# Weights 64 and 16 bytes past a multiple of 256 in a float32 decoder kernel

## The chip, the cores and the metric

The kernel runs on one core of a Trainium2 chip. The metric is the device time of one execution in microseconds. A core's engines work side by side and wait for one another by semaphores: TensorE (PE; PEld is its weight load), VectorE (DVE), ScalarE (ACT), GpSimd (POOL), and SyncE (SP), which here only issues transfers.

## The reference

A decoder trunk of two layers over 256 positions of width 2048, in float32. Cut to what matters here:

```python
h = _rmsnorm(x, nrm[0])
proj = h @ w_in_a[layer]                 # queries, keys, values; layer B has its own
...                                      # dilated windows (A) or stick-breaking (B), plus memory attention
x = x + _rmsnorm(heads @ w_o, norms[1])
u = _rmsnorm(x, norms[2]) @ w_up         # 2048 x 11264
gate, val = jnp.split(u, 2, axis=-1)
...                                      # causal convolution of width 3 on gate
f = (jax.nn.silu(acc) * val) @ w_down    # 5632 x 2048
x = x + _rmsnorm(f, norms[3])
```

Nearly all of the work is products of the 256 rows with large weight matrices, which are read from HBM once.

## The kernel before, in words

Each float32 operand is split into a high part, rounded to TensorE's `float32r`, and a low part, the rest. A product is then high x high + low x high + high x low, three matmuls. `split` makes the parts: ScalarE copies the loaded weights `raw` to `whi` (line 660), VectorE subtracts that from `raw` to `wlo` (line 661). Each pair of tiles holds 1024 columns of weights; there are four buffers of each.

Two forms of matmul use them, and in both a weight load (of the stationary operand, 128 columns) goes ahead of each matmul (which streams the moving operand).

In the activation-stationary form (`as_mm`, `mm3`, line 128) the weights move: 512 columns of `whi` or `wlo` stream past 128 columns of activations. It serves the values, the output and down projections, and, in `wide`, sums of blocks of weights (`forms`, tile `x`) and of activations.

In the weight-stationary form (`ws_mm`, line 145) 128 columns of `whi` or `wlo` are loaded and the activations move. `h` holds high and low parts of a block of 128 features side by side, so that one matmul of 512 columns gives high x high and high x low; one of 256 columns then gives low x high. A tile of 128 output features takes 16 such pairs. The weight-stationary tiles come in three places:

- `ws_tile`: 60 tiles, one after the other (queries, keys, the first group of the gated MLP and others); sums go to `ps_g`.
- `ws_beside`: 96 tiles, one in each unit of `wide`. A unit multiplies seven products of the activation-stationary form and one such tile, in halves of eight pairs between the products, pinned in program order. There are twelve stages of `wide` with eight units each. Sums go to `ps_s`.
- `mem_kv`: 64 pairs at the start, on weights from `piece`.

The program's order is written out by hand: `later` queues a step for a later tile, `behind_this` for the rest of a unit, and `pin` keeps what it wraps in program order. SyncE issues the loads of `raw`; GpSimd issues a load that adds to what lies in place (`first_sums`, line 668).

In SBUF `h1` and `h2` (the activations) begin at 77312 and 110080 in each partition, `whi` at 167424, 171520, 175616 and 179712, `wlo` at 183808 and then also every 4096. All of these are multiples of 256, and so are all steps of the two forms inside them: 512 bytes between weight loads, 1024 or 2048 between activations.

Of the kernel before, what the change touches and what calls it, by code (L numbers as in the profile page):

```python
# [11 lines left out]
F32R = mybir.dt.float32r  # L12
# [5 lines left out]
P = 128  # L18
# [18 lines left out]
WIDE = (1, 3, 5, 7, 9)  # L37


QK_ORDER = []  # L40
for _h in range(4):
    QK_ORDER += [("q", _h), ("q", 4 + _h), ("q", 8 + _h)]
    QK_ORDER += [("k", _h), ("k", 4 + _h), ("k", 8 + _h)]


class Body:
# [10 lines left out]
        return self.psp.tile([P, 512], F32, name="ps_" + tag, tag=tag, bufs=4)  # L57

    def small(self, n, dtype=F32):
        return self.sb.tile([P, n], dtype, name="small", tag="small", bufs=16)  # L60

    def sc(self, shape):
        return self.sb.tile(shape, F32, name="sc", tag="sc", bufs=4)
# [32 lines left out]
    def pin(self, ins):  # L96
        return self.tc.keep_in_program_order(ins) if self.pinned else ins


    def piece(self, src, cuts=1, store=None, between=None):  # L100


        nc = self.nc
        raw = self.sb.tile([P, 2048], F32, name="raw", tag="raw", bufs=3)
        n = 2048 // cuts
        for h in range(cuts):
            dma = nc.sync.dma_start(raw[:, h * n:(h + 1) * n], src[:, h * n:(h + 1) * n])
            if cuts > 1:
                self.tc.keep_in_program_order(dma)
            if h == 0 and between:  # L110
                between()
        res = []
        n = min(n, 1024)
        for h in range(2):
            if store:
                hi, lo = (v[:, h * 1024:(h + 1) * 1024] for v in store)
            else:
                hi = self.sb.tile([P, 1024], F32R, name="whi", tag="whi", bufs=4)
                lo = self.sb.tile([P, 1024], F32R, name="wlo", tag="wlo", bufs=4)
            for i in range(0, 1024, n):  # L120
                r, ns = raw[:, h * 1024 + i:h * 1024 + i + n], slice(i, i + n)
                did = self.split(hi[:, ns], lo[:, ns], r)
            res.append((hi, lo))
        self.splits.append(did)
        return res
# [7 lines left out]
    def ws_tile(self, out, src, h):  # L133


        b = self.bank()
        self.step()
        for half, (whi, wlo) in enumerate(self.piece(src)):
            for k in range(8):
                self.ws_mm(b, whi, wlo, k, h, half * 8 + k)  # L140
        self.ws_sum(out, b)
# [17 lines left out]
    def ws_beside(self, out, src, h, done=None):  # L159


        raw = self.sb.tile([P, 2048], F32, name="raw", tag="raw", bufs=3)
        self.pin(self.nc.sync.dma_start(raw, src))
        parts = []
        for i in range(2):
            parts.append([self.sb.tile([P, 1024], F32R, name=k, tag=k, bufs=4) for k in ("whi", "wlo")])
            self.split(*parts[i], raw[:, i * 1024:(i + 1) * 1024])
            yield
        b = self.bank("s")
        for half, (whi, wlo) in enumerate(parts):  # L170
            for k in range(8):
                self.ws_mm(b, whi, wlo, k, h, half * 8 + k, 7)
            yield
        self.ws_sum(out, b)
        if done:
            done()
# [495 lines left out]
    def wide(self, src, then, ahead, h, s, forms, r, beside, also, outs=None):  # L672

        nc, n = self.nc, KT // 2
        ps = {i: self.bank("g" if i in (1, 2, 6, 7) else "s") for i in range(1, 8)}
        pin, add = self.pin, nc.vector.tensor_add
        half = lambda f, i: f[..., i * 512:(i + 1) * 512]

        def lhs(i, u):
            if i in (1, 2, 4):
                kt, t = 2 * u + (i != 1), int(i == 4)
                return [h[2][:, kt, a, t * P:(t + 1) * P] for a in range(2)]  # L690
            return [s(u)[:, {5: 0, 6: 1, 7: 2, 3: 3}[i], a, :] for a in range(2)]

        def product(i, u, f, at):
            self.mm3(ps[i], *lhs(i, u), half(f[0], at), half(f[1], at), u == 0, u == n - 1)

        def load(u):

            raw = self.sb.tile([P, 2048], F32, name="raw", tag="raw", bufs=3)
            pin(nc.sync.dma_start(raw[:, :1536], src[u][:, :1536]))
            return raw  # L700

        def sums(d, raw):

            e = self.sh([P, 1024])
            pin(add(half(e, 1), half(d, 0), half(raw, 2)))
            pin(add(half(e, 0), half(e, 1), half(raw, 0)))  # L706
            return d, e

        def plain(raw):
            fa, fb = ([self.sb.tile([P, 1024], F32R, name=k, tag=k, bufs=4) for k in ("whi", "wlo")]  # L710
                      for _ in range(2))
            self.split(*fa, raw[:, 0:1024])
            self.split(*(half(f, 0) for f in fb), half(raw, 2))
            return fa, fb

        summed = [[forms[:, 2 * i + j, :] for j in range(2)] for i in range(2)]

        def split_sums(t):
            for of, parts in zip(t, summed):
                self.split(*parts, of)  # L720

        raw = load(0)

        high, low = self.splits[-4]
        with self.tc.issue_after(high.ins), self.tc.issue_after(low.ins):
            t = sums(ahead.pop(0), raw)
            split_sums(t)
        b = beside[0]()
        next(b)
        next(b)  # L730
        f = plain(raw)
        self.pinned = True
        for u in range(n):
            more = u + 1 < n
            next(b)
            if u:
                split_sums(t)
            self.catch_up()
            fa, fb = f
            product(1, u, fa, 1)  # L740
            product(2, u, fa, 0)
            product(3, u, fb, 0)
            if u + 2 < n:
                ahead.append(self.first_sums(src, u + 2))
            elif then is not None:
                ahead.append(self.first_sums(then, u + 2 - n))
            if more:
                raw = load(u + 1)
                after = beside[u + 1]()
                t, f = sums(ahead.pop(0), raw), plain(raw)  # L750
            self.catch_up()
            next(b)
            next(b, None)
            if more:
                next(after)
                next(after)
            if u in also:
                also[u]()
            product(7, u, summed[0], 1)
            product(5, u, summed[0], 0)  # L760
            product(6, u, summed[1], 1)
            product(4, u, summed[1], 0)
            b = after
        g0, a, v0, v1 = outs() if outs else (self.sc([P, 512]) for _ in range(4))
        more = lambda out, x, i: pin(add(out, ps[i], x))

        def scaled(out, i, t):
            pin(nc.vector.scalar_tensor_tensor(out, ps[i], r[:, t:t + 1], out, op0=ALU.mult, op1=ALU.add))

        pin(nc.scalar.copy(a, ps[1]))  # L770
        pin(nc.scalar.activation(g0, ps[1], AF.Copy, scale=r[:, 0:1]))  # L771
        scaled(g0, 2, 0)
        more(a, a, 6)
        more(v0, a, 5)
        more(v0, v0, 3)
        more(a, a, 7)
        more(v1, a, 5)
        pin(nc.scalar.activation(a, a, AF.Copy, scale=r[:, 1:2]))
        scaled(a, 4, 1)
        self.pinned = False  # L780
        self.catch_up(-1)
        return (g0, a), (v0, v1)
# [264 lines left out]
    def run(self):  # L1047
# [105 lines left out]
        def pair(j, out):  # L1153
            who = QK_ORDER[2 * j:2 * j + 2]
            for i, w in enumerate(who):
                tiles[w] = out[:, i, :]
            return self.rotate(out, [w[0] for w in who])
# [182 lines left out]
def _layout(i):  # L1340
# [6 lines left out]
    heads_a = wa.reshape(D, 40, E)  # L1347
    order = [(0 if k == "q" else 12) + h for k, h in QK_ORDER]

# [41 lines left out]
```

## Time and profile before

| | |
|---|---|
| median of 3 runs | 2173.35 us (2172.65 to 2173.58) |
| the profiled execution | 2173.27 us, of which the span from the first to the last instruction is 2171.5 us |
| granted TensorE clock | 0.999 of full speed |
| PE / PEld / DVE / ACT / POOL busy | 2157.3 / 1823.0 / 1734.3 / 1329.2 / 175.6 us |
| matmuls of line 128 and of line 145 | 5100 and 5120 of 10926 |
| HBM read and written | 510.17 and 26.74 MB, 247 GB/s over the span |

A matmul's duration in the profile includes the way through the array, so that the durations of neighbours overlap; the time that one takes from the next is read from start to start, or from a piece of the chain of waits, which gives the length and the count of matmuls in a row. Changes of a duration in a row of equal matmuls show as changes of that step.

### The profile page before, as it was taken

Reading aid. Unit: us, or ns where it says so; the run is one execution under the profiler, and the core shown is the slowest. Engines: PE = TensorE matmul, PEld = TensorE weight load, DVE = VectorE, ACT = ScalarE, POOL = GpSimd, SP = SyncE. Lnnn points to the kernel's source line nnn. Section 1 sums busy time; section 2 is a strip of 40 time slices with the busy share of each in tenths; the row PEclk is TensorE's granted clock in tenths of the full one; section 3 lists DMA queues with packets and bytes.
Section 4 is the critical chain, followed back from the end, with each engine's and each line's share of the span. In section 5 each row is a group of like instructions: output and inputs, shape, how many; then the busy total and the mean of one; then the engine's idle time right before and its main releaser. Section 6 shows DMA issues by size and latency. Waiting matters only on the chain.

```text
span 2171.5 us, 29241 instructions
## 1 busy us (share of the span) xinstructions
PE 2157.3 (99%) x10926; PEld 1823.0 (84%) x10926; DVE 1734.3 (80%) x2350; ACT 1329.2 (61%) x1896; POOL 175.6 (8%) x201
## 2 busy tenths in 40 slices
PE   9999999999999999999999999999999999999998
PEld 8888888888888888888888888878888888888887
DVE  7798867997887868778888877569978878687786
ACT  6666756666665666666675655456666656666563
POOL 0000001010101011010111000010101010110100
PEclk9999999999999999999999999999999999999999
DMA  9886557796979879797778744577969798897974
GB/s 369 251 260 246 175 180 258 224 277 223 298 233 283 265 235 297 227 288 254 268 266 259 251 163 169 194 238 225 279 227 287 234 282 269 237 298 221 288 247 182
DMA packets 111775, 538.83 MB, mean 248 GB/s; under 512 B 11280, under 2 KB 11664, under 8 KB 73488
## 3 DMA queue, kind: packets, MB, share of 16 engines
q1 hardware_dynamic: 75744, 445.66, 57.0%
q0 software_dynamic: 35744, 91.24, 21.0%
q8 instruction: 86, 1.41, 0.2%
q14 instruction: 57, 0.47, 0.1%
q10 hardware_dynamic: 144, 0.06, 0.0%
HBM read 510.17 MB, written 26.74 MB: 247 GB/s over the span
## 4 chain that ended last, share of the span: by engine, by line
PE 97%; DVE 1%; issue 1%; DMA 1%; ACT 0%; POOL 0%; SPq 0%; POOLq 0%; DVEq 0%; ACTq 0%
PE ps_g L128 40%; PE ps_s L145 26%; PE ps_g L145 15%; PE ps_s L128 11%; PE ps_s L953 1%; PE ps_s L278 1%; PE ps_s L354 0%; PE ps_s L381 0%; DMA sh<-in_uw_dram 0%; DVE wlo L661 0%; DMA raw<-in_wmv_dram 0%; PE ps_s L486 0%; PE ps_s L468 0%; PE ps_s L526 0%; PE ps_s L425 0%
## 5 line engine op out<-in xcount | busy, mean ns | idle before, releaser
L661 DVE TENSOR_TENSOR wlo<-raw,whi 128x1024 fp32r<-128x1024 f32 (+1 forms) x758 | 854.9, 1151 | 251.0 <-ACT whi L660 243.5
L660 ACT CAST whi<-raw 128x1024 fp32r<-128x1024 f32 (+1 forms) x758 | 743.5, 996 | 392.7 <-PE ps_g L128 145.1
L145 PE MATMUL ps_s<-h,whi 128*128 128x512 f32 x1600 | 580.3, 397 | 0.0
L128 PE MATMUL ps_g<-whi,sh 128*128 128x512 f32 x1488 | 461.5, 391 | 0.5 <-ACT sc L771 0.5
L145 PE MATMUL ps_s<-h,wlo 128*128 128x256 f32 x1600 | 417.1, 281 | 0.1
L145 PEld LDWEIGHTS ps_s<-h,whi 128*128 128x128 f32 x1600 | 300.4, 188 | 59.1
L145 PE MATMUL ps_g<-h,whi 128*128 128x512 f32 x960 | 342.5, 401 | 0.8 <-DVE h L268 0.8
L128 PEld LDWEIGHTS ps_g<-whi,sh 128*128 128x128 f32 x1488 | 277.3, 188 | 57.6 <-ACT sc L771 1.4
L145 PEld LDWEIGHTS ps_s<-h,wlo 128*128 128x128 f32 x1600 | 301.7, 189 | 25.4 <-DVE wlo L661 0.7
L128 PE MATMUL ps_g<-wlo,sh 128*128 128x512 f32 x744 | 289.9, 390 | 0.0
L145 PE MATMUL ps_g<-h,wlo 128*128 128x256 f32 x960 | 259.5, 281 | 0.0
L661 DVE TENSOR_TENSOR x<-sh,x 128x1024 fp32r<-128x1024 f32 x192 | 227.0, 1219 | 0.1
L128 PE MATMUL ps_g<-whi,h 128*128 128x512 f32 x688 | 214.2, 392 | 0.6 <-ACT whi L660 0.6
L145 PEld LDWEIGHTS ps_g<-h,whi 128*128 128x128 f32 x960 | 178.6, 188 | 39.2 <-DVE h L268 1.1
L660 ACT CAST x<-sh 128x1024 fp32r<-128x1024 f32 x192 | 193.0, 1051 | 1.8 <-DVE sh L706 1.8
L145 PEld LDWEIGHTS ps_g<-h,wlo 128*128 128x128 f32 x960 | 181.2, 189 | 4.5
L156 ACT COPY qk<-ps_s 128x256 f32<-128x256 f32 x96 | 35.9, 374 | 227.3 <-PE ps_s L145 227.3
L128 PEld LDWEIGHTS ps_g<-wlo,sh 128*128 128x128 f32 x744 | 139.7, 188 | 29.3
L128 PE MATMUL ps_s<-x,h 128*128 128x512 f32 x552 | 155.3, 390 | 0.0
L668 POOL DMA_DIRECT2D sh<-in_uw_dram x80 | 98.4, 1229 | 659.7 <-DMA sh<-in_uw_dram 274.1
L128 PE MATMUL ps_g<-x,h 128*128 128x512 f32 x528 | 149.7, 391 | 0.0
L128 PEld LDWEIGHTS ps_g<-whi,h 128*128 128x128 f32 x688 | 128.9, 188 | 24.4 <-ACT whi L660 1.0
(215 smaller groups left out, 2253.3 us busy)
## 6 DMA issues: line engine op xcount, KB each, us to landing
raw<-in_up_dram SPq DMA_DIRECT2D x96, 1024.0 KB, 7.0
raw<-in_dn_dram SPq DMA_DIRECT2D x88, 1024.0 KB, 5.5
raw<-in_uw_dram SPq DMA_DIRECT2D x80, 768.0 KB, 7.9
sh<-in_uw_dram SPq DMA_DIRECT2D x80, 512.0 KB, 8.2
sh<-in_uw_dram POOLq DMA_DIRECT2D x80, 512.0 KB, 10.5
raw<-in_wqk_a_dram SPq DMA_DIRECT2D x24, 1024.0 KB, 5.0
yout<-sh POOLq DMA_DIRECT2D x32, 512.0 KB, 8.7
raw<-in_wo_b_dram SPq DMA_DIRECT2D x16, 1024.0 KB, 4.9
```

What stands on the lines that cost most here:

```text
L128: mm = lambda *o, **k: self.pin(self.nc.tensor.matmul(*o, **k))
L145: mm = lambda *o, **kw: self.pin(self.nc.tensor.matmul(*o, **kw))
L156: self.pin(self.nc.scalar.copy(out, b[:, S:]))
L278: self.nc.tensor.transpose(b[:, k * S + t * P:k * S + (t + 1) * P], self.x[:, t, kt * P:(kt + 1) * P], self.ident)
L660: high = self.pin(self.nc.scalar.copy(hi, of))
L661: low = self.pin(self.nc.vector.tensor_sub(lo, of, hi.bitcast(F32)))
L668: self.nc.gpsimd.dma_start(d.rearrange("p (a n) -> p a n", a=2), src[u][:, 1536:].unsqueeze(1).to_broadcast([P, 2, 512]), accum_op=ALU.add)
L953: nc.tensor.transpose(b[:, j * S + t * P:j * S + (t + 1) * P], of[t][:, f:f + P], self.ident)
```

## The change

In the weight-stationary tiles of `ws_tile` and `ws_beside` the weights' tiles get 64 more columns, and the 1024 columns that are used begin 16 elements (64 bytes) into `whi` and 4 elements (16 bytes) into `wlo`. Everywhere else (`as_mm`'s moving weights, `plain` in `wide`, and `mem_kv`) they begin at 0. The buffers are then 4352 bytes apart, 17 x 256. To make room, the ring of `small` (a few columns of row sums, maxima and the like) has 11 buffers instead of 16. The instructions of each engine and their order are as before; with fewer `small` buffers, one exponential of ScalarE in the first layer's attention waits for GpSimd in addition.

```diff
+APART = (16, 4)
...
     def small(self, n, dtype=F32):
-        return self.sb.tile([P, n], dtype, name="small", tag="small", bufs=16)
+        return self.sb.tile([P, n], dtype, name="small", tag="small", bufs=11)
...
+    def halves(self, at=(0, 0)):
+        both = []
+        for name, o in zip(("whi", "wlo"), at):
+            both.append(self.sb.tile([P, 1088], F32R, name=name, tag=name, bufs=4)[:, o:o + 1024])
+        return both
+
-    def piece(self, src, cuts=1, store=None, between=None):
+    def piece(self, src, cuts=1, store=None, between=None, at=(0, 0)):
...
-                hi = self.sb.tile([P, 1024], F32R, name="whi", tag="whi", bufs=4)
-                lo = self.sb.tile([P, 1024], F32R, name="wlo", tag="wlo", bufs=4)
+                hi, lo = self.halves(at)
...  (ws_tile)
-        for half, (whi, wlo) in enumerate(self.piece(src)):
+        for half, (whi, wlo) in enumerate(self.piece(src, at=APART)):
...  (ws_beside)
-            parts.append([self.sb.tile([P, 1024], F32R, name=k, tag=k, bufs=4) for k in ("whi", "wlo")])
+            parts.append(self.halves(APART))
...  (wide, plain)
-            fa, fb = ([self.sb.tile([P, 1024], F32R, name=k, tag=k, bufs=4) for k in ("whi", "wlo")]
-                      for _ in range(2))
+            fa, fb = self.halves(), self.halves()
```

## The prediction, made before the change was run

> **What bounds the kernel now.** I read the busy times first, then the chain of waits (whole span, then pieces of it), then the groups of instructions, and last stretches of time.
>
> ```profile
> PE 2157.3 (99%) x10926; PEld 1823.0 (84%) x10926; DVE 1734.3 (80%) x2350; ACT 1329.2 (61%) x1896; POOL 175.6 (8%) x201
> by line: PE ps_g L128 40.2%; PE ps_s L145 25.7%; PE ps_g L145 15.5%; PE ps_s L128 11.5%; PE ps_s L953 0.8%; issue 0.7%; PE ps_s L278 0.6%; PE ps_s L354 0.3%; PE ps_s L381 0.3%; DMA sh<-in_uw_dram 0.3%; DVE wlo L661 0.3%; DMA raw<-in_wmv_dra
> ```
>
> TensorE is the chain: lines 128 and 145 alone are 92.9% of it, and what waits for VectorE or a transfer is a few tenths of a per cent each. Line 145 is the weight-stationary matmul, which the change touches: 25.7 + 15.5 = 41.2% of 2171.5 us, 895 us. Line 128 has the activations as weights and isn't touched. So the question is what one matmul of line 145 costs beyond what it must, and the pieces of the chain tell it, since each gives a length and a count:
>
> ```profile
> 310.27 32.69 PE ps_g L128 x144
> 1378.63 54.24 PE ps_g L128 x239
> ...
> 544.05 2.81 PE ps_s L145 x16
> ...
> 200.04 5.65 PE ps_g L145 x32
> ...
> 187.77 11.29 PE ps_g L145 x64
> 263.04 11.11 PE ps_g L145 x64
> ```
>
> (start, length in us, what, count.) On line 128 a 512-column matmul takes 32.69 / 144 = 227.0 ns and 54.24 / 239 = 226.9 ns, over hundreds in a row. Line 145 alternates 512 columns (high weights) with 256 (low weights). At the same rate a pair would take 227 + 113.5 = 340.5 ns. It takes 2.81 / 8 = 351 ns, 5.65 / 16 = 353 ns, 11.29 / 32 = 353 ns and, at best, 11.11 / 32 = 347 ns. None of these pieces holds a wait for another engine. So a pair loses 7 to 13 ns inside TensorE. The views by line show the same loss in single instructions (minimum/median/maximum in ns; then mean in the groups):
>
> ```profile
> L128 PE MATMUL ps_s<-whi,h x176: 389/389/389, 100.8 to 2089.5; 128*128 128x512 f32 x176
> ...
> L145 PE MATMUL ps_s<-h,whi x1600: 388/396/403, 12.9 to 2092.5; 128*128 128x512 f32 x178
> L145 PE MATMUL ps_s<-h,wlo x1600: 277/281/384, 13.1 to 2092.4; 128*128 128x256 f32 x178
> ...
> L145 PE MATMUL ps_g<-h,whi x960: 387/395/586, 73.6 to 1496.3; 128*128 128x512 f32 x192
> L145 PE MATMUL ps_g<-h,wlo x960: 274/280/467, 73.9 to 1496.2; 128*128 128x256 f32 x192
> ```
>
> On line 128, 176 matmuls of 512 columns all last 389 ns. On line 145 the same width lasts 388 to 403, and 256 columns 277 to 284 or so. The loss: 1600 x (396 - 389) = 11.2 us, 960 x (395 - 389) = 5.8 us (medians, because the longest here hold real waits), 1600 x (281 - 277.5) = 5.6 us, 960 x (280 - 277.5) = 2.4 us (277.5 is the untouched length: the minimum of the row, half a nanosecond rounded in). Sum 25.0 us. By the pieces, 2560 x (351 to 353 - 340.5) is 27 to 32 us, less where pieces run at 347. I take 27 us, 10.5 ns a pair. That is all that an edit of line 145's operands can win at this streaming rate.
>
> What makes the loss? Beside each matmul runs the load of the next weights, and it isn't the longer partner:
>
> ```profile
> L145 PEld LDWEIGHTS ps_s<-h,wlo x1600: 186/189/190, 13.1 to 2092.3; 128*128 128x128 f32 x178
> L145 PEld LDWEIGHTS ps_s<-h,whi x1600: 187/188/191, 12.7 to 2092.4; 128*128 128x128 f32 x178
> ...
> 580.73 0.40 PE L145 MATMUL ps_s<-h,whi 128*128 128x512 f32 x1
> 580.98 0.28 PE L145 MATMUL ps_s<-h,wlo 128*128 128x256 f32 x1
> 581.10 0.40 PE L145 MATMUL ps_s<-h,whi 128*128 128x512 f32 x1
> ```
>
> A load lasts 188 to 189 ns with its latency, on line 128 and here alike. From start to start the 512-column matmul took 0.25 us here and the 256-column one 0.12 (227 and 113.5 would be the untouched steps). The wide matmul has most of the loss although one load fits well into 227 ns. So the loss isn't a load that is too long; it looks like two reading streams that get in each other's way. In such a case the weights' place against the moving operand's can matter, and here both always start at multiples of 256 bytes. Line 128 has that alignment too and loses next to nothing, so alignment alone doesn't decide: with equal widths the two streams fall into step, with 512 and 256 in turn they don't.
>
> **The change, part by part.** No instruction is added, removed or moved; each engine issues the same operations in the same order, and no DMA changes.
>
> (1) Weights of `ws_tile` and `ws_beside`: 156 of the 160 tiles' worth of line 145. The 64 pairs of `mem_kv` keep the old place (its `piece` is called without `at`), so 2560 - 64 = 2496 pairs change. The trace of before holds no other alignment of these operands, so the effect is bounded by rows. Best: the whole 10.5 ns goes, 2496 x 10.5 = 26 us. Worst: every pair takes the longest steady lengths, 403 ns (its row's maximum) and 284 ns (281 plus as much as it lies above the minimum), so (403 - 389) + (284 - 277.5) = 20.5 ns instead of 10.5, +10 x 2496 = +25 us. Between them lies the 347 ns of the piece at 263.04, that is 6.5 ns lost with today's alignment, only met in another phase; landing there would win 4 x 2496 = 10 us. Today's usual 351 to 353 ns is the bad end of what the same addresses show (347 to 353), so a new meeting of the streams is likelier to be better than worse. I take the middle between 6.5 ns left and none left: 10 and 26 us, 18 us.
>
> (2) Splits. ScalarE writes the high part 64 bytes past, VectorE reads it there and writes the low part 16 bytes past.
>
> ```profile
> L864 DVE SCALAR_TENSOR_TENSOR qk<-qk,cols 128x254 f32<-128x254 f32 x88 | 42.2, 482 | 2.4
> L864 DVE SCALAR_TENSOR_TENSOR qk<-qk,cols 128x255 f32<-128x255 f32 x88 | 42.0, 480 | 10.6 <-ACT qk L857 10.3
> ...
> L268 DVE SCALAR_TENSOR_TENSOR h<-sh,cols,h 128x256 fp32r<-128x256 f32 x64 | 27.1, 480 | 5.1 <-ACT h L267 5.0
> ```
>
> Line 864 writes 8 and 4 bytes past its tile's start and takes 482 and 480 ns; the same operation from a tile's start takes 480. So I cost it at nothing. ScalarE's writes have no such row; 5% on the 1053 ns of a split would be 50 ns, under a ScalarE that is 61% busy. What covers both is TensorE's 99%; the cover is thinnest on VectorE in the wide stages, next.
>
> (3) What is late next. In the wide stages, where 96 of the tiles are, the other resources are near full:
>
> ```profile
> core 0: us, PE busy (x) PEld busy (x) DVE busy (x) ACT busy (x) POOL busy (x), PEclk, DMA share, GB/s
> 414.60:495.00 80.40, 80.40 (x412) 67.86 (x411) 74.88 (x102) 50.19 (x64) 8.41 (x7) 1.00 0.94 283
> ...
> 672.60:753.10 80.50, 80.50 (x413) 67.94 (x412) 67.49 (x81) 49.36 (x62) 9.36 (x8) 1.00 0.98 297
> 930.10:1010.50 80.40, 80.40 (x412) 67.88 (x411) 67.40 (x81) 49.33 (x62) 6.94 (x6) 1.00 0.89 269
> ```
>
> Such a stage holds 8 tiles, 128 pairs: 128 x 10.5 = 1.3 us at most of 80.4. VectorE with 74.9 us still fits in 79.1. The DMA engines with 0.98 x 80.5 = 78.9 us just fit. With half the gain nothing fills up. I take 1 us off over all stages for queues that grow.
>
> (4) `small` has 11 buffers instead of 16; it holds a few columns of sums. The rows that use it are hidden: its GpSimd power takes 753 ns x 8, and before these GpSimd had waited 178.5 us, so nobody waits for it:
>
> ```profile
> L237 POOL TENSOR_TENSOR small<-small,mhalf 128x1 f32<-128x1 f32 x8 | 6.0, 753 | 178.5 <-DVE small L235 178.5
> ```
>
> An earlier reuse adds one wait of ScalarE for GpSimd in the first layer's attention; if that were a whole power late, it would be 0.8 us. I take 0.
>
> (5) The moving high and low weights of line 128 stay at multiples of 256, only 4352 bytes apart instead of 4096: 0.
>
> Sum against the profiled execution: 2173.27 - 18 + 1 = 2156. The median of the runs, 2173.35, is the same within 0.1 us. I predict 2156 us.
>
> **The rivals.** (a) Nothing happens. For it: 347 and 353 ns occur with the same alignment, so timing alone may decide; and line 128, also at multiples of 256, runs clean. If the streams meet in one shared port and not in a place, an address can't help: 2173, within 4 us.
> The Trainium skill, "TensorE: Matmul & The Clock Gate" (Step-by-step: what each phase is for), says that the moving operand and the weights come through two independent read ports and that loading the next weights takes nothing from the running matmul. By that rule the time is 2173 too; the rows above speak against its full form, since 389 ns becomes 396 where only the interplay differs, but they don't show that the address is the reason.
>
> (b) Slower. The low weights are loaded while the 512-column matmul streams, 16 bytes past the grid on which that operand lies; if this shifts the two streams into the worst meeting, each pair loses the 20.5 ns of (1): 2173 + 25 = 2198. It decides from the point where the mean loss of a pair exceeds today's 10.5 ns; 12.5 ns would be 2178. For it: 403 ns stands in the row. Against: it is one step of three there, and today's mean is already near the bad end.
>
> (c) TensorE gets faster and the wide stages wait for transfers. If the four or so stages at 0.94 to 0.98 win nothing and the others all they can, 26 - 4 x 1.3 = 21 us is left, 2152 to 2153: it caps the good case, no more.
>
> **How the numbers follow.** Faster by a real amount, with (c) in it: 0.62, between 2164 (6.5 ns left) and 2147 (none left). A little lower is possible: line 128 loses some microseconds where it follows line 145 and must fall into step again (below: median 389 ns by line, mean 391 in the groups); 5 us of that would make 2142.
>
> ```profile
> L128 PE MATMUL ps_g<-whi,sh x1488: 387/389/580, 294.2 to 2118.6; 128*128 128x512 f32 x186
> ...
> L128 PE MATMUL ps_g<-whi,sh 128*128 128x512 f32 x1488 | 461.5, 391 | 0.5 <-ACT sc L771 0.5
> ```
>
> (a) has 0.16, around 2173. (b) has 0.22, from 2178 to 2198; the half of it nearer to today ends at 2187. The range is 2142 to 2187. Within the likeliest case it is 2142 to 2165. Changes below 0.2% (4.3 us) can't be told from none.
>
> **What would show it.** Right: the pieces of line 145 in the chain fall from 351 to 353 ns a pair towards 341 to 347; the median of the 512-column row falls from 396 towards 389 and of the 256-column one from 281 towards 278; line 128 stays at 227; the span falls by what 2496 pairs lose. Splits at 1222 and 1053 ns stay as they are. (a): medians of 396 and 281 unchanged. (b): medians over 398, or LDWEIGHTS over 190. Wrong in a way that I don't weigh: a streaming rate other than 227 ns for 512 columns on line 145, or splits that take longer and starve TensorE, which the waits of line 145 for VectorE would show.

## The result, and the profile after

| | before | after |
|---|---|---|
| median | 2173.47 us | 2161.36 us |
| lowest and highest | 2172.65, 2174.02 | 2161.30, 2161.89 |
| span of the profiled execution | 2171.5 us | 2159.6 us |

The change makes the kernel 12.1 us faster: a ratio of 0.9945, 95% interval 0.993 to 0.996. Forecast were 2156 us in a range of 2142 to 2187, and faster with 0.62.

The code has nine lines more, so line 128 is now 137 (weights move), line 145 is 154 (weights stand), and the splits 660 and 661 are 669 and 670. Busy times and the chain of waits of the changed kernel:

```profile
PE 2146.0 (99%) x10926; PEld 1823.1 (84%) x10926; DVE 1732.9 (80%) x2350; ACT 1328.2 (62%) x1896; POOL 175.4 (8%) x201
...
by line: PE ps_g L137 40.5%; PE ps_s L154 25.5%; PE ps_g L154 15.4%; PE ps_s L137 11.5%; PE ps_s L961 0.8%; issue 0.7%; PE ps_s L287 0.6%; PE ps_s L363 0.3%; PE ps_s L390 0.3%; DMA sh<-in_uw_dram 0.3%; DVE wlo L670 0.3%; PE ps_s L1082 0.3%;
```

TensorE's busy time fell by 11.3 us; the other engines' didn't move. The share of line 154 fell from 41.2% of 2171.5 us to 40.9% of 2159.6 us, 894.7 to 883.3 us: 11.4 us, nearly all of the change. (A tenth of a per cent is 2.2 us here, so this is rough; the starts of matmuls below are the better measure.) Pieces of the chain, start, length and count, in a wide stage and in tiles one after the other:

```profile
545.03 2.79 PE ps_s L154 x16
547.82 0.70 PE ps_g L137 x3
550.55 2.79 PE ps_s L154 x16
...
581.65 2.75 PE ps_s L154 x16
584.40 1.38 PE ps_g L137 x6
586.45 2.79 PE ps_s L154 x16
...
591.98 2.75 PE ps_s L154 x16
596.79 2.79 PE ps_s L154 x16
...
186.54 11.02 PE ps_g L154 x64
...
307.75 32.67 PE ps_g L137 x144
340.42 16.68 PE ps_g L154 x96
```

Eight pairs were 2.81 us and are 2.75 or 2.79 now. Of the rows of 16, those at 545.03, 586.45 and 596.79 are second halves of tiles and the others first halves: 2.75 occurs in first halves alone. Tiles in a row go from 353 ns a pair to 11.02 / 32 = 344 and 16.68 / 48 = 347.5. Line 137 stays at 32.67 / 144 = 226.9 ns. By line (minimum/median/maximum):

```profile
L154 PE MATMUL ps_s<-h,whi x1600: 388/393/404, 12.5 to 2080.6; 128*128 128x512 f32 x178
L154 PEld LDWEIGHTS ps_s<-h,wlo x1600: 185/188/193, 12.5 to 2080.4; 128*128 128x128 f32 x178
L154 PE MATMUL ps_s<-h,wlo x1600: 275/281/386, 12.7 to 2080.5; 128*128 128x256 f32 x178
L154 PEld LDWEIGHTS ps_g<-h,whi x960: 186/188/193, 73.0 to 1487.4; 128*128 128x128 f32 x192
L154 PE MATMUL ps_g<-h,whi x960: 388/392/588, 73.2 to 1487.5; 128*128 128x512 f32 x192
```

The 512-column matmul's median fell from 396 to 393 and from 395 to 392; the 256-column one's stayed at 281. So what was won lies in the matmul of the high weights, beside which the low weights are loaded, and a loss is left in both.

For the experiments I take the loss from the starts of matmuls in the trace. A clean step is 226.7 ns for 512 columns and 113.3 ns for 256 (the mean of long quiet rows of line 128, and half of it). What a step takes beyond that, up to 20 ns, is counted as loss; longer ones are taken for waits for other engines and left out. Sums over each kernel, in us:

| kernel | place of high, low (bytes) | 512 columns, line 145 | 256 columns, line 145 | line 128 | sum | against before | measured |
|---|---|---|---|---|---|---|---|
| before | 0, 0 | 19.9 | 8.9 | 5.1 | 33.9 | | |
| after | 64, 16 | 9.0 | 8.3 | 5.2 | 22.5 | -11.4 | -12.1 |
| padding alone | 0, 0 | 20.1 | 8.8 | 5.4 | 34.3 | +0.4 | +0.1 |
| high alone | 64, 0 | 10.1 | 7.7 | 4.8 | 22.6 | -11.3 | -11.9 |
| low alone | 0, 16 | 12.7 | 10.0 | 8.7 | 31.4 | -2.5 | -2.6 |
| whole 256 | 256, 256 | 20.1 | 8.8 | 5.5 | 34.4 | +0.5 | +0.3 |
| h2 moved too | 64, 0 from h2 | 8.8 | 7.5 | 11.1 | 27.4 | -6.5 | -7.0 |
| high at 192 | 192, 0 | 5.7 | 4.8 | 1.2 | 11.7 | -22.2 | -22.7 |

The losses inside TensorE account for each measured time within 0.7 us, so nothing else has to be looked for.

### The profile page after: what moved, and what is told of

The parts are those of the page before. It is cut to its first block, busy times and chain, and to the rows that moved or that the text cites. A ratio compares the mean times of both kernels' runs of the same rounds, so it can differ in the third digit from the quotient of the medians.

```text
span 2159.6 us, 29240 instructions
## 1 busy us (share of the span) xinstructions
PE 2146.0 (99%) x10926; PEld 1823.1 (84%) x10926; DVE 1732.9 (80%) x2350; ACT 1328.2 (62%) x1896; POOL 175.4 (8%) x201
## 4 chain that ended last, share of the span: by engine, by line
PE 97%; DVE 1%; issue 1%; ACT 0%; DMA 0%; POOL 0%; POOLq 0%; DVEq 0%; SPq 0%; ACTq 0%
PE ps_g L137 40%; PE ps_s L154 25%; PE ps_g L154 15%; PE ps_s L137 12%; PE ps_s L961 1%; PE ps_s L287 1%; PE ps_s L363 0%; PE ps_s L390 0%; DMA sh<-in_uw_dram 0%; DVE wlo L670 0%; PE ps_s L1082 0%; PE ps_s L495 0%; PE ps_s L477 0%; PE ps_s L535 0%; PE ps_s L434 0%
## 5 line engine op out<-in xcount | busy, mean ns | idle before, releaser
L154 PE MATMUL ps_s<-h,whi 128*128 128x512 f32 x1600 | 573.3, 393 | 0.0
L154 PE MATMUL ps_g<-h,whi 128*128 128x512 f32 x960 | 338.0, 396 | 0.8 <-DVE h L277 0.8
## 6 DMA issues: line engine op xcount, KB each, us to landing
sh<-in_uw_dram POOLq DMA_DIRECT2D x80, 512.0 KB, 10.4
```

The costliest lines, as they stand in the source:

```text
L154: mm = lambda *o, **kw: self.pin(self.nc.tensor.matmul(*o, **kw))
```

## The experiments

My theory going in (A): beside each matmul the next weights are read, and the place of these weights within 256 bytes, against the moving operand, decides how often the two streams hold each other up. The main rival (B): any new layout re-deals the timing.

**Padding alone, high alone, low alone, and both by 256 bytes.** Each is the changed kernel with another constant:

```diff
-APART = (16, 4)
+APART = (0, 0)      # padding alone
+APART = (16, 0)     # high alone
+APART = (0, 4)      # low alone
+APART = (64, 64)    # both by 256 bytes
```

> Both offsets 0, but the tiles padded to 4352 bytes and the ring of small at 11 as in the changed kernel. Theory A (the place of the weights within 256 bytes, against the moving operand, decides how the two streams meet): as the kernel before, 2173 us within 1; eight pairs of a wide stage 2.81 us; median of the 512-column matmul of the weight-stationary form 396 ns. Rival B (any new layout or the changed ring moves the phase, the place within 256 bytes doesn't count): as the changed kernel, 2161 us, 2.75 to 2.79 us.

> Both offsets 256 bytes, so that all weights are again at multiples of 256, in other rows of memory. Theory A: as before, 2173 us within 1, because only the place within 256 bytes counts. Rival B: some other value, such as 2161. Rival C (any distance between weights and the grid of the other tiles helps, whole multiples of 256 too): 2161.

Measured: 2173.59 us, ratio 1.0002 (0.9993 to 1.0011), and 2173.75 us, ratio 1.0002 (0.9992 to 1.0011). The row of the run with 256 bytes is the old one:

```profile
L154 PE MATMUL ps_s<-h,whi x1600: 388/396/403, 13.4 to 2093.3; 128*128 128x512 f32 x178
L154 PE MATMUL ps_s<-h,wlo x1600: 277/281/384, 13.7 to 2093.1; 128*128 128x256 f32 x178
```

B falls, and rival C with it: padding, other rows of memory and the shorter ring of `small` change nothing. To move both weights by 256 bytes doesn't count; moves within 256 bytes do, as follows.

> High weights 64 bytes past a multiple of 256, low weights at 0. The high weights are loaded beside the 256-column matmul, the low ones beside the 512-column matmul. Theory A1 (each load meets the stream beside it by itself): the high weights hold the smaller part, so the loss of the 256-column steps goes and 9 of 29 us at most: 2170 us. Theory A2 (the low weights' 16 bytes do all): 2173. Rival A3 (the 64 bytes do all): 2161.

> Low weights 16 bytes past a multiple of 256, high weights at 0. Theory A1: the low weights, loaded beside the 512-column matmul, hold the larger part of what was won (its steps fell by 10.9 us, the 256-column ones by 0.6): 2162 to 2164 us. A2: 2161. A3: 2173.

Measured: 2161.63 us, ratio 0.9948 (0.9931 to 0.9964), with the high weights alone; 2170.89 us, ratio 0.9987 (0.9978 to 0.9996), with the low alone. A1 falls, and with it my idea that a load is held up by, and holds up, just the matmul beside it: to move the high weights, which are loaded beside the 256-column matmul, took 9.8 us from the 512-column steps. The two forms hang together. The trace of before already showed that "beside" was too narrow: the load of high weights at 544.12 us starts with a 256-column matmul and is recorded with 0.19 us, while the next 512-column matmul starts 0.11 us later. A3 (the 64 bytes do all) had 2161 and 2173 and is the nearest, but the low weights alone still win 2.6 us, and the two gains don't add up. Half tiles of a wide stage with the high weights alone:

```profile
545.60 2.75 PE ps_s L154 x16
551.09 2.81 PE ps_s L154 x16
555.95 2.75 PE ps_s L154 x16
561.44 2.75 PE ps_s L154 x16
...
566.24 2.75 PE ps_s L154 x16
571.73 2.81 PE ps_s L154 x16
576.59 2.75 PE ps_s L154 x16
```

Each second row is the first half of a tile (551.09, 561.44, 571.73): 2.81 or 2.75. All second halves are 2.75. So the same place ends in several steady states. I counted them: the mean loss of a pair in the inner part of each half tile, in cycles of 0.833 ns (starts are recorded in whole ns; in this unit the most frequent means come out as 8, 12 and 16). The wide stages have 96 first and 96 second halves, the tiles in a row 60 and 60.

| place | wide, first halves | wide, second halves | tiles in a row, second halves |
|---|---|---|---|
| 0, 0 (before) | 16 (94), 10 (2) | 16 (all) | 16 (38), 8 (20) |
| 64, 16 (after) | 0 to 2 (55), 8 to 10 (41) | 8 to 10 (all) | 0 (15), 8 (44) |
| 64, 0 | 0 to 4 (35), 12 to 16 (61) | 0 (all) | 0 (16), 12 (28), 16 (16) |
| 0, 16 | 10 to 11 (94), 8 (1), 16 (1) | 11 (all) | 16 (14), 8 (44) |
| 192, 0 (below) | 0 to 5 (94), 12 (2) | 0 (all) | 0 (47), 12 (12) |

(One or two half tiles that hold a wait, or are in no listed state, are left out of the last column.) So the pairs run into a repeating pattern, and the place offers a few such patterns. With 0, 0 they lose 16 or 8 cycles a pair (13 or 7 ns); with 64, 16 they lose 8 to 10 or next to none; with 64, 0 none or 12 to 16. That 64, 16 and 64, 0 take the same time is chance: they are different mixtures of states.

What ran before a half tile seems to choose the pattern: first and second halves of one place follow different products and end differently. No run changed that alone for line 154. For line 128 (137 here) the run with the low weights alone does: its own places are the old ones, and yet it loses 8.7 us instead of 5.1. Behind a half tile of a wide stage its first eight matmuls lose 38 ns there, where in the kernel before the first four lost 20 ns.

**Is it the unequal widths?** In the kernel before, all 512 columns also meet the low weights; that adds low x low to the sum.

```diff
-        mm(b[:, 0:S], wlo[:, ks], one, start=False, stop=False)
+        mm(b, wlo[:, ks], both, start=False, stop=False)
```

> The kernel before, all operands at multiples of 256, but the low weights too are met by all 512 columns (high and low activations), so that both matmuls of a pair are 512 wide. It adds the product low x low to the sum. If unequal widths are what keeps the streams out of step, a pair takes 2 x 227 = 454 ns with no loss, though the places are as before: 2173 + 2560 x (454 - 351) ns = 2437 us, and the medians are 389 ns in both forms. If the place alone makes the loss, it stays or doubles: 2437 + 29 = 2466 us, medians 396 ns.

Measured: 2430.62 us. All operands lie at multiples of 256, and the loss is gone:

```profile
L145 PE MATMUL ps_s<-h,whi x1600: 388/389/398, 12.7 to 2350.2; 128*128 128x512 f32 x178
L145 PE MATMUL ps_s<-h,wlo x1600: 389/389/398, 12.9 to 2349.9; 128*128 128x512 f32 x178
L145 PE MATMUL ps_g<-h,whi x960: 387/389/583, 79.8 to 1690.4; 128*128 128x512 f32 x192
```

By starts line 145 loses 2.7 us in all and line 128 1.0 (5.1 before, mostly the first steps behind line 145). The fall on line 128 makes about 4 of the 6 us under the expected 2437, and waits for other engines, the longer steps left out above, fell by 2.4 us more (12.1 to 9.7); the 2.7 us that line 145 still loses and the rounding of 454 and 351 ns about cancel. At this place equal streams fall into step and stay there, and 512 and 256 in turn never do. The load itself isn't too long: it lasts 188 ns in both.

**Sixteen places in one kernel.** The place goes round from tile to tile; the wide stages count their tiles apart from the tiles in a row.

```diff
+def apart(n):
+    return (4 * (n % 16), 0)        # scan of the high weights
+    return (16, 4 * (n % 16))       # scan of the low weights, high at 64
+    return (48, 4 * (n % 16))       # the same, high at 192
+    return (44 + n % 9, 0)          # fine scan of the high weights
...
-        for half, (whi, wlo) in enumerate(self.piece(src, at=APART)):
+        at = apart(self.nth[0])
+        self.nth[0] += 1
+        for half, (whi, wlo) in enumerate(self.piece(src, at=at)):
...  (ws_beside, with its own count)
-            parts.append(self.halves(APART))
+            parts.append(self.halves(at))
```

> The place of the high weights goes round from tile to tile: 0, 16, 32 ... 240 bytes past a multiple of 256, low weights at 0; tiles of the wide stages and tiles in a row are counted apart, so that each place comes six times in the wide stages and three or four times in a row. Known ends: place 0 loses 16 cycles of 1.2 GHz a pair (13 ns) in the wide stages, place 64 loses 2 (half tiles in step) to 9. Theory A (the load of the next weights meets the running stream at fixed places of a line of memory of some width): the loss repeats with that width, so 64 looks like 128 and 192 if the line is 64 bytes - but then 64 could not differ from 0 -, hence the width is 128 or 256: with 128, 192 is like 64, and 128 like 0; with 256, neither. Rival D (only the distance counts, the farther the better): the loss falls steadily from 0 to 128 and rises again. Time between 2161 and 2173 by either.

> High weights at 64 bytes for every tile, the place of the low weights goes round as before: 0, 16 ... 240 bytes. Known: place 0 has second half tiles in step (2 cycles a pair, first halves 9), place 16 has first halves mostly in step and second halves at 9. Theory A: the low weights' place decides in which of the two states (in step, or 8 cycles a pair lost) a half tile ends, with the same width of the line as in the scan of the high weights. Rival D: one place is best and the loss grows with the distance from it. Rival E (the low weights' place doesn't matter, only what ran before a half tile does): first and second halves change places with no order in them. Time 2157 to 2170.

Measured: 2168.02 and 2168.05 us, one execution each. Mean loss of a pair in the wide stages, first and second halves, in cycles:

| place | high, low at 0 | low, high at 64 | low, high at 192 |
|---|---|---|---|
| 0 | 14.6, 16.0 | 0.0, 0.0 | 0.1, 0.2 |
| 16 | 11.0, 11.7 | 3.5, 8.9 | 9.5, 15.9 |
| 32 | 14.9, 14.7 | 11.1, 13.4 | 9.4, 10.3 |
| 48 | 12.1, 11.4 | 13.0, 12.7 | 11.0, 12.1 |
| 64 | 0.0, 0.0 | 14.3, 14.2 | 16.9, 16.3 |
| 80 | 11.6, 9.9 | 11.8, 11.5 | 8.7, 8.2 |
| 96 | 9.7, 8.2 | 15.1, 13.8 | 12.3, 10.3 |
| 112 | 10.4, 10.2 | 9.6, 9.7 | 10.6, 11.3 |
| 128 | 12.8, 14.2 | 12.3, 12.1 | 8.6, 8.1 |
| 144 | 9.4, 11.3 | 10.2, 13.0 | 2.4, 13.4 |
| 160 | 9.4, 11.3 | 9.7, 16.5 | 12.6, 12.0 |
| 176 | 13.8, 13.8 | 9.3, 8.0 | 10.2, 11.2 |
| 192 | 2.0, 0.1 | 14.3, 12.2 | 15.3, 10.6 |
| 208 | 9.6, 15.3 | 11.3, 13.8 | 8.0, 10.0 |
| 224 | 7.7, 4.6 | 13.1, 11.3 | 10.8, 10.8 |
| 240 | 10.5, 12.0 | 4.7, 5.5 | 7.1, 9.6 |

(The third column is a run told of below.) With low at 0 the high weights' places 64 and 192 are nearly without loss, 128 and 0 are bad. On these four places that is the period of 128 bytes of theory A, but the period isn't shown: other places 128 bytes apart, such as 32 and 160, 80 and 208 or 96 and 224, differ by 2 to 6 cycles, and the low weights lose 0 at place 0 and 12 at 128. Rival D falls: 48 and 80, next to 64, lose 10 to 12. For the low weights with the high ones at 64, place 0 is best, then 240 and 16; theory A had only two states there, in step or 8, and up to 16.5 were measured. Rival E falls too: in this run second halves of one place agree within 0.4 cycles, while those of different places lie between 0 and 16.5. (Each place always follows the same other place here, so the run doesn't show what another one ahead of it would do.)

**Against the moving operand, or absolute?** The activations `h2` begin 64 bytes later, which moves `whi` and `wlo` by 64 as well; the high weights get 64 on top.

```diff
+        o = 16 if which == "h2" else 0
-        h = self.sb.tile([P, KT, 2, S], F32R, name=which, tag=which, bufs=1)
+        whole = self.sb.tile([P, KT * 2 * S + o], F32R, name=which, tag=which, bufs=1)
+        h = whole[:, o:].rearrange("p (k a s) -> p k a s", k=KT, a=2)
...
-APART = (16, 4)
+APART = (16, 0)
```

> The activations h2 begin 64 bytes past a multiple of 256, and all buffers of whi and wlo too; on top of that the high weights lie 64 bytes further in weight-stationary tiles. So against the moving h2 the weights lie as in the run with only the high weights moved, while all absolute places are others. (small has 9 buffers for room.) Theory A (the place against the moving operand counts): wide tiles as there, 2.73 us for eight pairs in second halves, and the weight-stationary part as at 2161.6 us. Rival F (the absolute place counts): high at 128 and low at 64, another value. The activation-stationary matmuls, where whi and wlo now move at 64 past and the activations of sh and h1 stay at 0: if what moves had to lie at multiples of 256, or both together, their 227 ns for 512 columns grow, by A and F alike up to the 236 ns seen before a fall into step, 10 us or more; if a stream of equal widths falls into step whatever the places, they stay and the whole is 2161.

Measured: 2166.79 us, ratio 0.9967 (0.9955 to 0.9980). In the wide stages all 96 second halves lose nothing, as with the high weights alone, though the absolute places are 128 and 64: the place against the moving operand counts. Tiles in a row on `h1`, which stayed at 0 and is met from 128 and 64, lose 7 to 11 instead of 0, 12 or 16. The old line 128, now 139, is slower here. In a large part of it the weights now move at 64 past, and the activations (`sh`, or sums in `h1`) are at 0:

```profile
L139 PE MATMUL ps_g<-whi,sh x1488: 387/392/586, 293.8 to 2112.6; 128*128 128x512 f32 x186
L139 PE MATMUL ps_s<-whi,h x176: 391/393/395, 101.1 to 2083.3; 128*128 128x512 f32 x176
```

389 ns became 392 and 393. As 392 is the median of 1488 matmuls, it isn't the entry alone. The line loses 11.1 us instead of the 4.8 with the high weights alone, 6.3 us more; 4.3 of them are in the products with `sh`. The weight-stationary line loses 1.5 us less, and the kernel is 5.2 us slower. I had expected 10 us or more, or none: a stream of equal widths can lose by its place too, and the price is smaller than I thought.

**A place with few bad states.** The scan of the high weights had no bad state in twelve half tiles at 192. It had none at 64 either, where the run with 64 alone had 61 of 96 first halves at 12 to 16; so only a run of its own could tell the two apart.

```diff
-APART = (16, 4)
+APART = (48, 0)
```

> High weights 192 bytes past a multiple of 256, low weights at 0, otherwise the changed kernel. In the scan of the high weights 0.1 to 2 cycles a pair were lost at this place, in half tiles of all twelve entries, where 64 bytes had both 0 (there) and 12 to 16 (in the run of its own, first halves). Theory A with several steady states: a place is good if every entry ends in step, so nearly all of the 29 us goes but what falling into step costs (some 6 us): 2150 us. Rival G (64 and 192 are alike, and the entries of the scan were lucky): states of 12 to 16 cycles come back in first halves and tiles in a row, 2161. Rival H (the split writes at other places cost): waits of line 154 for VectorE or ScalarE, none seen so far.

> High weights at 192 bytes, the low weights' place goes round as before. With the high weights at 64 the low weights had to be at 0 (0 cycles), 16 (0 or 9) or 240 (5); all else lost 8 to 16. Theory A: the same pattern with 192, with losses near 0 only at low places 0, 16 and 240, or its mirror image. Rival E: no order. Time 2157 to 2170.

Measured with 192 and 0: 2150.80 us, ratio 0.9893 (0.9876 to 0.9909) against before; it is the fastest of all and 10.6 us faster than the change as made. (Its profiled execution took 2152.17 us.)

```profile
L154 PE MATMUL ps_s<-h,whi x1600: 387/389/403, 12.7 to 2071.2; 128*128 128x512 f32 x178
L154 PE MATMUL ps_s<-h,wlo x1600: 276/276/384, 12.9 to 2071.0; 128*128 128x256 f32 x178
```

The medians are the clean ones, 389 and 276. Of 28.8 us on line 145 10.5 are left, in the first steps of half tiles and in the tiles in a row that end at 12. The scan of the low weights with the high ones at 192 (2166.78 us; third column above) has 0 as the one good place; 16 and 240, good or fair with 64, lose 7 to 16 here, so the expected pattern didn't come.

> High weights at 176, 180, 184 ... 208 bytes past a multiple of 256, from tile to tile in turn, low weights at 0: how exact must the place be? Known from steps of 16: 192 loses 0 to 2 cycles a pair, 176 and 208 lose 10 to 15. Theory I (memory is read in lines of 16 bytes, and only the line counts in which an operand starts): 192, 196, 200 and 204 lose the same, 176 to 188 the same, with a jump at 192. Rival K (the loss rises with the distance in steps of 4 bytes): a valley around 192, 188 and 196 alike at some cycles. Time 2160 to 2170.

Measured: 2169.51 us. Loss in cycles, first and second halves:

| 176 | 180 | 184 | 188 | 192 | 196 | 200 | 204 | 208 |
|---|---|---|---|---|---|---|---|---|
| 14.4, 14.8 | 9.0, 15.7 | 9.5, 8.0 | 11.6, 9.2 | 1.5, 0.1 | 9.4, 8.4 | 11.4, 8.0 | 2.8, 1.5 | 10.7, 15.3 |

Both I and K fall: four bytes beside 192 cost 8 cycles, and 204 is nearly as good as 192. There is neither a line of 16 bytes in it nor a valley. States hide in these means: first halves at 180 lose 0 to 15.6 cycles, second halves at 196 7.6 to 15.4. Why these places and no others stays open; I have no model of the two streams that gives the table.

## Why the prediction was right, and where it was off

**The bound and the loss.** That the loss lies between the matmuls and the loads of the next weights was argued from 389 against 396 ns on the same width. The runs bear it out: with equal widths nearly all of it goes at the old places, and with unequal widths the place of the weights, which TensorE reads only in these loads, takes up to 18.3 us of it away. Its size, forecast with 27 us, was 28.8 by starts.

**Term (1), 18 us, was mis-sized; it is 11.4.** I had taken the middle between 6.5 ns left a pair and none. The step that was off is this choice. What is left is 17.3 us on 2560 pairs, 6.8 ns: the end that the piece at 263.04 of the kernel before had shown. The table of states gives the main reason. That piece was two tiles in the state of 8 cycles, 6.7 ns, and with 64, 16 all second halves of the wide stages and most tiles in a row end in this state or one close to it. I had read it as a sample out of a range that goes on to zero; it was one of two clusters of lengths, 8 and 16 cycles, which sorting the tiles in a row by length would have shown. That the mean comes out so near to it is partly chance: the inner pairs lose 3.5 ns in first halves, 7.4 in second halves and 5 to 6 in a row, and first pairs of half tiles and the unchanged `mem_kv` add the rest. One sign that I had named didn't come: the 256-column median stayed at 281 instead of falling towards 278.

The sentence that a new meeting is likelier better than worse held, for all other places of the high weights' scan lose less than 16 in the mean. But how much 64 would win was luck in part: the scans over sixteen and over nine places win only 4 to 6 us, 64 is one of the few places near zero, and the prediction had no reason from the place itself.

**Terms (2) to (5).** The splits cost nothing at their new places, and the addition that writes 8 and 4 bytes in is unchanged too:

```profile
L670 DVE TENSOR_TENSOR wlo<-raw,whi 128x1024 fp32r<-128x1024 f32 x658 | 793.8, 1222 | 244.6 <-ACT whi L669 231.4 <-PE ps_g L137 6.5 <-PE ps_s L961 1.8
L669 ACT CAST whi<-raw 128x1024 fp32r<-128x1024 f32 x658 | 680.7, 1051 | 378.2 <-PE ps_g L137 145.8 <-PE ps_s L154 118.9 <-issue 58.9
```

1222 ns before and after, 1053 and 1051. Padding and `small` cost nothing: 2173.59 us. The reading that nobody waits for the power of `small` was wrong, though. That GpSimd had waited before it says nothing of who waits behind it, and in the kernel before VectorE does:

```profile
L560 DVE SCALAR_TENSOR_TENSOR x<-sh,small,x 128x512 f32<-128x512 f32 x32 | 22.1, 746 | 1.2 <-POOL small L237 1.1
```

All waits for it come to 2.9 us before and 2.7 after, so the change didn't lengthen them. The 1 us taken off for queues that grow was not needed; the transfers fill the stage that had 0.98, and still TensorE is busy throughout:

```profile
core 0: us, PE busy (x) PEld busy (x) DVE busy (x) ACT busy (x) POOL busy (x), PEclk, DMA share, GB/s
411.20:491.00 79.80, 79.80 (x411) 67.81 (x410) 74.92 (x101) 50.38 (x65) 8.41 (x7) 1.00 0.94 286
...
667.00:746.50 79.50, 79.50 (x409) 67.55 (x408) 66.17 (x79) 49.70 (x62) 9.36 (x8) 1.00 1.00 300
```

With 192 and 0 the same stage takes 79.2 us, so rival (c) had not begun to bind.

**Rivals.** (a) is out: the place moves the time by up to 22.7 us. The rule of the Trainium skill that was weighed there ("TensorE: Matmul & The Clock Gate", Step-by-step: what each phase is for: loading the next weights takes nothing from the running matmul) fits the rows of equal widths at multiples of 256, 389 ns beside a load each, and doesn't fit 512 and 256 columns in turn, where 28.8 us are lost and up to 18.3 of them hang on where the weights lie. (b) gave the low weights' 16 bytes the deciding part; they have the smaller one, and the high weights' 64 bytes decide. A pair at 20.5 ns, 25 cycles, never became a steady state; the worst seen in any half tile of the scans is 17 cycles.

**Line 128.** That it might lose less behind a line 145 in step, some 5 us, didn't come with 64, 16 (5.1 and 5.2 us), but did with 192, 0 (1.2 us).

## What to carry to other kernels

Where matmuls of unequal widths take turns with fresh weights each, compare their duration with that of a uniform stream; a few per cent above it without a wait (here 396 against 389 ns) can be the two operand streams holding each other up. Try the place of the weights against the moving operand, one place for each tile in a single kernel, and read the loss tile by tile. Then give each good place a run of its own, as a scan doesn't show every entry, and take the one that ends in step from most. A pattern that repeats has few states: sort the lengths before taking a middle between them.

## What the runs showed of the hardware that was not expected

- Pairs of matmuls in the same place have two or three steady losses, such as 8 and 16 cycles of 0.833 ns at 0, 0, or 0, 12 and 16 at 64, 0, and keep the one they entered through the inner pairs of a half tile.
- Moving the weights that are loaded beside the 256-column matmul changed the 512-column steps by 9.8 us and the 256-column ones by 1.2.
- Places four bytes apart differ by 8 cycles a pair (192 and 196), and to move both weights by 256 bytes changes nothing (2173.75 against 2173.49 us).
- Equal widths at unchanged places need longer to fall into step behind other half tiles: eight matmuls and 38 ns with the low weights moved, four and 20 ns before.
- The DMA engines' share reached 1.00 in a stage of 79.5 us without a wait of TensorE.
